# A gMLP and dilated-attention trunk on one core: combined weights and low halves moved to VectorE, a left operand read back from DRAM, attention steps moved out of the v stage

## The chip, the cores and the metric

The kernel runs on one core of a Trainium2 chip. The metric is the device time of one execution in microseconds (us). Five engines take part, each with an instruction stream of its own that runs in order: TensorE (PE; its weight loads are shown apart as PEld), VectorE (DVE), ScalarE (ACT), GpSimd (POOL), and SyncE (SP), which issues nearly all DMA transfers. Engines wait for each other through semaphores.

## The reference

The input is x, 2048 tokens by D = 1024, float32. There are two layers, cut here to what the kernel must compute:

```
h = rms_norm(x) * (1 + scale) + shift          # ada_mod(c) gives shift, scale, gate
u, v, z = split(h @ w_in, 3)                   # w_in: 1024 x 6144
v = rms_norm(gelu(v))
mixed = einsum('gts,bcsge->bctge', tril(w_s), v) + b_s    # inside chunks of 128 tokens
x1 = x + gate * ((gelu(u) * mixed * silu(z)) @ w_out)     # w_out: 2048 x 1024

k, v = split(norm(x1) @ w_kv)                  # one shared K/V, 6 heads of 128
q, z = norm(x1) @ w_in                         # 24 query heads, and 1024 columns of z
# three groups of 8 heads with dilation 1, 4 and 16, each over a band of 128 + own positions,
# with ALiBi slopes; the three outputs are weighed by softmax of their log-sum-exp
out = x1 + gate * ((sum_g alpha_g * o_g) * silu(z)) @ w_out
```

## The kernel before

**Tiling.** The tokens are worked in NQ = 4 quarters of QT = 512. A quarter runs `layer_A` (the gMLP layer) and then `proj_B` (K/V and queries of the attention layer); `finish` closes the last layer after the fourth quarter. `layer_A` has four stages, each of which keeps TensorE busy for 90 to 130 us: v, u, z and o (the product with w_out). Every float32 product is made of three TensorE products of high and low halves: `split` (L244) lets ACT copy a tile to its high half (L246) and another engine subtract that from the tile for the low half (L247). `mm3` (L275) issues the three.

**v in quarters 1 to 3** is made by `dense_s`, a Strassen-Winograd scheme with 7 products in place of 8 for each of two column blocks (numbers 4 and 5 of `block_of`). A product is 24 matmuls of 128x512 over four weight tiles, which `wunits` loads by SP and splits. The scheme needs combined weights (t1 to t4) and sums of the left operand (s1 to s4). `combine_weights` makes the former once, four 128x512 operations on POOL for each of 8 quads (L349 to L352), and stores them in DRAM (`wt`); for blocks 4 and 5 (`where="sums"`) this happens in quarter 0, mostly in the o stage. `sums_A` makes the latter: POOL adds the high and low halves of h, four tiles of 128x1024 (L610), DVE makes the sums (L614 to L617), and ACT and DVE split them into sA. In v the argument `shared=True` gives the low half of a product's fourth weight tile to POOL.

**h** itself is made by `norm_T` (names h_a, hAh, hAl) for the next quarter while `proj_B` runs; L489 writes it, L491 copies the high half, L493 (POOL) subtracts.

**Fillers.** Attention of the quarter before (`attend_local`, 80 steps) is a generator. The dense stages call `tick`, which advances the generators by `rate` steps for every full tick. The rate is 1.0 in v (16 ticks) and 1.5 or, in quarter 2, 1.6 in u, z and o (48 ticks); what is left is drained at the end of o. One attention visit is spread over four rounds: transposes of q and k (pq, pk), scores (ps, L1043 to L1049), transposes of the probabilities (pp, L1090 and L1104), and the product with v (po). Between scores and pp stand DVE's bias and maximum (L1052 to L1056), ACT's exponential (L1062) and POOL's diagonal, mask and copy (L1070 to L1073). In quarter 2 `ada_gate` "gb" (sums of a gate, DMA loads and DVE operations) is a second filler beside it.

**Order.** The tile framework's scheduler turns the program into one order per engine by priorities; engines and SP's queue then run in that order. The start of u also holds the scaling of v: eight DVE operations of 128x1024 (L780), each after a row factor rv from POOL, ahead of the mixing product pm (L787).

The line numbers in this document are those of the kernel before, unless a sentence says after: there a line stands one to five lower (L248 of after is L247, L351 to L354 are L349 to L352, L785 is L780, L1057 is L1052, L1095 is L1090).

Of the kernel before, what the change touches and what calls it, by code (L numbers as in the profile page):

```python
# [18 lines left out]
P = 128  # L19
# [15 lines left out]
def trunk(ctx, tc, out, x, c, a_ada_w, a_ada_b, a_norm_g, a_w_in, a_sgu_g, a_w_spatial,  # L35
# [27 lines left out]
    std = [dp.tile([S, 16], F32, name=f"std{g}") for g in range(3)]  # L63
    zd = dp.tile([S, D], F32, name="zd")
    gd = dp.tile([2, D], F32, name="gd")
    wt = [[dp.tile([512, 512], F32, name=f"wt{b}_{i}") for i in range(4)] for b in range(6)]

    fillers = []
# [172 lines left out]
        nc.gpsimd.tensor_tensor(t[:, 0:n], t[:, 0:n], mhalf[:, 0:n], ALU.pow)  # L241
        return t

    def split(hi, lo, src, e=None):  # L244

        nc.scalar.activation(hi, src, AF.Copy)  # L246
        (e or nc.vector).tensor_tensor(lo, src, hi.bitcast(F32), ALU.subtract)  # L247

    def wunits(w, k0, n0, nm, nk=KT, ordered=False, shared=False):
        us = []  # L250
        for kk in range(nk):
            u = wp.tile([P, 2, 512], F32R, tag="w", name=f"w_{nm}{kk}")
            raw = rp.tile([P, 512], F32, tag="raw", name=f"raw_{nm}{kk}")
            ld = nc.sync.dma_start(raw, w[(k0 + kk) * P:(k0 + kk + 1) * P, n0:n0 + 512])
            last_ld[0] = ld
            if ordered:
                tc.keep_in_program_order(ld)
            split(u[:, 0, :], u[:, 1, :], raw, nc.gpsimd if shared and kk == nk - 1 else None)
            us.append(u)
        return us  # L260

# [62 lines left out]
    def combine_weights(blocks, where):  # L324


        todo = [(b, k) for b in blocks for k in range(4)]
        quads = {}

        def load(i):  # L330
            b, k = todo[i]
            w, n0 = block_of(b)
            q = quads[i] = []
            for r in range(2):
                if where == "sums" or where == "both" and i % 2:
                    t = [sum_tile(f"cw{b}{k}{r}{c}")[:, 0:512] for c in range(2)]
                    for c in range(2):
                        nc.sync.dma_start(t[c], w[(4 * r + k) * P:(4 * r + k + 1) * P,
                                                  n0 + c * 512:n0 + (c + 1) * 512])
                else:  # L340
                    t = xp.tile([P, 2, 512], F32, tag="xin", name=f"cw{b}{k}{r}")
                    nc.sync.dma_start(t, w[(4 * r + k) * P:(4 * r + k + 1) * P, n0:n0 + D]
                                      .rearrange("p (c n) -> p c n", c=2))
                    t = [t[:, c, :] for c in range(2)]
                q += t

        def combine(i):
            t1, t3, t4, t2 = quads[i]
            nc.gpsimd.tensor_tensor(t1, t3, t1, ALU.subtract)  # L349
            nc.gpsimd.tensor_tensor(t3, t2, t3, ALU.subtract)  # L350
            nc.gpsimd.tensor_tensor(t2, t2, t1, ALU.subtract)  # L351
            nc.gpsimd.tensor_tensor(t4, t4, t2, ALU.subtract)  # L352

        def store(i):  # L354
            b, k = todo[i]
            t1, t3, t4, t2 = quads.pop(i)
            for j, t in enumerate((t1, t2, t3, t4)):
                nc.sync.dma_start(wt[b][j][k * P:(k + 1) * P, :], t)
            if k == 3:
                combined.add(b)  # L360

        for i in range(len(todo) + 2):
# [15 lines left out]
    def sum_tile(nm):  # L378
        return tp.tile([P, 520], F32, tag="st", name=f"st_{nm}")

    def dense_s(ops, b, nm, evac, late=None, shared=False):


        x, y = ([pst(f"pd_{nm}{c}{i}", "d") for i in range(2)] for c in "ab")
# [5 lines left out]
        src.update({f"t{i + 1}": (wt[b][i], 0, 0) for i in range(4)})  # L390

        def product(pts, a, w, first):
            us = wunits(*src[w], f"{nm}{w}_", 4, shared=shared)
# [76 lines left out]
    def norm_T(xts, pr, outs, nm, ks=range(0, KT, 2), act=False):  # L470

        tok = slice(pr * 256, pr * 256 + 256)
        pts = {}
        for oi, (hh, hl, a, b) in enumerate(outs):
            for k2 in ks:
                if oi == 0:
                    pts[k2] = pst(f"pt_{nm}{k2}").rearrange("p (k t) -> p k t", k=2)
                    for kk in range(2):
                        for i in range(2):
                            last = nc.tensor.transpose(pts[k2][:, kk, i * P:(i + 1) * P],  # L480
                                                       xts[i][:, (k2 + kk) * P:(k2 + kk + 1) * P], ident)
                h = evt(f"h_{nm}{k2}_{oi}").rearrange("p (k t) -> p k t", k=2)
                for kk in range(2):
                    k = k2 + kk
                    if act or (oi == 1):
                        nc.scalar.activation(h[:, kk, :], pts[k2][:, kk, :], AF.Identity,
                                             scale=a[:, k:k + 1], bias=b[:, k:k + 1])
                    else:
                        nc.vector.tensor_scalar(h[:, kk, :], pts[k2][:, kk, :], a[:, k:k + 1],  # L489
                                                b[:, k:k + 1], ALU.mult, ALU.add)  # L490
                nc.scalar.activation(hh[:, k2:k2 + 2, tok], h, AF.Copy)  # L491
                e = nc.vector if oi == 0 and len(outs) > 1 else nc.gpsimd
                e.tensor_tensor(hl[:, k2:k2 + 2, tok], h,  # L493
                                hh[:, k2:k2 + 2, tok].bitcast(F32), ALU.subtract)
        return last
# [100 lines left out]
    def sums_A(Q, hA, m):  # L596
# [9 lines left out]
            f[n] = m[1][:, i, :].rearrange("p (k t) -> p k t", k=4)  # L606
        for n in ("11", "21", "22", "12"):
            k, c = part[n]
            hi, lo = (h[:, k:k + 4, c:c + 256].bitcast(F32) for h in hA)
            nc.gpsimd.tensor_tensor(f[n], hi, lo, ALU.add)  # L610
        s = {"s1": f["22"], "s3": f["21"], "s2": f["11"], "s4": f["12"]}

        def sums():
# [761 lines left out]
```

## Time and profile before

| what | value |
|---|---|
| three runs | 3020.75, 3022.59, 3026.84 us (median 3022.59) |
| profiled execution, its own time | 3020.51 us |
| span of its profile | 3018.5 us |
| mean granted TensorE clock | 0.994 |
| v stage, quarters 1, 2, 3 (on TensorE) | 648 to 742, 1292 to 1391, 1967 to 2067 us |
| o stage of quarter 0 | 324 to 421 us |

The span is the time from the first to the last record; the profiled execution's own time holds 2.0 us more. The granted clock is the share of full speed that TensorE was allowed. A wait is idle time of an engine ahead of an instruction; the profile puts it down to the instruction that released it last ("A <- B" reads: A waited for B, or A is made from B).

### The profile page before, as it was taken

The numbers are of one execution on the slowest core, as the hardware profiler recorded it, in microseconds if no ns is written. First come the engines' busy times: TensorE is split into PE (matmuls) and PEld (weight loads), VectorE is DVE, ScalarE is ACT, GpSimd is POOL, SyncE is SP. The second block draws the span as 40 slices with busy tenths as digits, with TensorE's granted clock in tenths as the row PEclk, the third lists the DMA queues.
The fourth block names the chain that finished last, engine by engine and source line by source line (L and its number), as shares of the span: only waits on it lengthen the run. The fifth ranks groups of instructions, "written<-read, shape, count | busy, mean of one in ns | idle before, by whom it ended". The sixth has DMA issues, their size and how long they took to land. (4 is left out here: it accounts for less than half of the span.)

```text
span 3018.5 us, 45519 instructions
## 1 busy us (share of the span) xinstructions
PE 2937.2 (97%) x14752; PEld 2453.0 (81%) x14752; DVE 2125.0 (70%) x3714; ACT 1664.4 (55%) x3397; POOL 904.3 (30%) x1130
## 2 busy tenths in 40 slices
PE   7999999999999999999999999999999999999999
PEld 4788788878888888877888888878888888977787
DVE  5877566787557576887657686887577576878672
ACT  4323355768556365675445366576455366867440
POOL 1057422442003213643213213543123111122322
PEclk9999999999999999999999999999999999999999
DMA  8899865766343466765333366765433466788652
GB/s 275 274 310 346 295 229 180 254 218 194 120 130 102 126 200 213 254 219 164 107 121 124 116 199 210 252 195 158 131 101 106 133 194 203 235 279 293 214 168 91
DMA packets 363265, 583.49 MB, mean 193 GB/s; under 512 B 38442, under 2 KB 137996, under 8 KB 363028
## 3 DMA queue, kind: packets, MB, share of 16 engines
q1 hardware_dynamic: 363028, 580.59, 59.9%
q8 instruction: 117, 1.92, 0.3%
q14 instruction: 120, 0.98, 0.1%
HBM read 466.54 MB, written 113.91 MB: 192 GB/s over the span
## 5 line engine op out<-in xcount | busy, mean ns | idle before, releaser
L275 PE MATMUL pd_o<-w_o,yh 128*128 128x512 f32 x1024 | 322.1, 395 | 5.3 <-DVE w_o L247 5.3
L275 PE MATMUL pd_kv<-w_kv,hkh 128*128 128x512 f32 x768 | 239.1, 393 | 0.3
L275 PEld LDWEIGHTS pd_o<-w_o,yh 128*128 128x128 f32 x1024 | 190.7, 189 | 44.6 <-DVE w_o L247 6.3
L1062 ACT ACTIVATE pr<-pr,stat,rt 128x256 f32<-128x256 f32 (+1 forms) x320 | 177.6, 557 | 85.6 <-DVE stat L1059 54.3
L313 PE MATMUL pd_u<-hAh,w_u 128*128 128x512 f32 x512 | 206.7, 404 | 0.0
L313 PE MATMUL pd_z<-hAh,w_z 128*128 128x512 f32 x512 | 204.2, 399 | 0.0
L275 PE MATMUL pd_o<-w_o,yl 128*128 128x512 f32 x512 | 201.0, 393 | 0.0
L315 PE MATMUL pd_u<-hAh,w_u 128*128 128x512 f32 x512 | 200.4, 391 | 0.0
L315 PE MATMUL pd_z<-hAh,w_z 128*128 128x512 f32 x512 | 200.4, 391 | 0.0
L314 PE MATMUL pd_z<-hAl,w_z 128*128 128x512 f32 x512 | 199.8, 390 | 0.0
L314 PE MATMUL pd_u<-hAl,w_u 128*128 128x512 f32 x512 | 199.8, 390 | 0.0
L246 ACT ACTIVATE w_z<-raw_z 128x512 fp32r<-128x512 f32 x128 | 79.2, 628 | 173.4 <-PE pd_z L315 64.2
L275 PEld LDWEIGHTS pd_kv<-w_kv,hkh 128*128 128x128 f32 x768 | 143.0, 188 | 30.6 <-ACT hkh L519 2.0
L246 ACT ACTIVATE w_u<-raw_u 128x512 fp32r<-128x512 f32 x128 | 79.0, 629 | 160.9 <-PE pd_u L315 74.9
L246 ACT ACTIVATE w_o<-raw_o 128x512 fp32r<-128x512 f32 x128 | 79.2, 628 | 144.9 <-PE pd_o L275 66.2
L247 DVE TENSOR_TENSOR w_z<-raw_z,w_z 128x512 fp32r<-128x512 f32 x128 | 100.9, 797 | 78.0 <-ACT w_z L246 77.6
L1070 POOL TENSOR_TENSOR dg<-pr,ident 128x256 f32<-128x256 f32 x76 | 60.7, 798 | 314.3 <-ACT pr L1062 302.4
L1123 PEld LDWEIGHTS po<-kv,pT 128*128 128x128 f32 x1200 | 147.5, 192 | 8.1 <-ACT pT L970 1.6
L1123 PE MATMUL po<-kv,pT 128*128 128x128 f32 x1200 | 149.7, 275 | 1.0 <-ACT pT L970 1.0
L275 PE MATMUL pd_kv<-w_kv,hkl 128*128 128x512 f32 x384 | 149.6, 391 | 0.0
L247 DVE TENSOR_TENSOR w_o<-raw_o,w_o 128x512 fp32r<-128x512 f32 x128 | 100.9, 799 | 68.2 <-ACT w_o L246 68.1
L1052 DVE SCALAR_TENSOR_TENSOR pr<-dist,rt,ps 128x256 f32<-128x256 f32 (+1 forms) x320 | 122.6, 429 | 22.1 <-PE ps L1049 17.3
(837 smaller groups left out, 8177.0 us busy)
## 6 DMA issues: line engine op xcount, KB each, us to landing
raw_q<-in_b_w_in_dram SPq DMA_DIRECT2D x144, 256.0 KB, 3.3
raw_u<-in_a_w_in_dram SPq DMA_DIRECT2D x128, 256.0 KB, 3.6
raw_z<-in_a_w_in_dram SPq DMA_DIRECT2D x128, 256.0 KB, 3.3
raw_o<-in_a_w_out_dram SPq DMA_DIRECT2D x128, 256.0 KB, 3.0
qt<-qd SPq DMA_DIRECT2D x96, 260.0 KB, 3.2
raw_v<-in_a_w_in_dram SPq DMA_DIRECT2D x96, 256.0 KB, 4.0
raw_kv<-in_w_kv_dram SPq DMA_DIRECT2D x96, 256.0 KB, 3.1
od<-ot SPq DMA_DIRECT2D x96, 256.0 KB, 3.2
```

Source lines behind the costliest of these rows:

```text
L246: nc.scalar.activation(hi, src, AF.Copy)
L247: (e or nc.vector).tensor_tensor(lo, src, hi.bitcast(F32), ALU.subtract)
L275: last_mm[0] = nc.tensor.matmul(pt, a, u[:, w, :], start=f, stop=e, skip_group_check=more)
L313: nc.tensor.matmul(pts[i], wh, hh[:, k, :], start=k == 0, stop=False)
L314: nc.tensor.matmul(pts[i], wh, hl[:, k, :], start=False, stop=False)
L315: nc.tensor.matmul(pts[i], wl, hh[:, k, :], start=False, stop=k == KT - 1)
L1052: nc.vector.scalar_tensor_tensor(pr[:, i, :], dist[:, 256 - w:256], u["rt"][:, h:h + 1], psc[:, i, :], ALU.mult, ALU.add)
L1062: nc.scalar.activation(pr[:, i, :], pr[:, i, :], AF.Exp, bias=mneg[:, i:i + 1], scale=u["rt"][:, h:h + 1], accum_out=lsum[:, i:i + 1])
L1070: nc.gpsimd.tensor_tensor(dg, prev, ident.unsqueeze(1).broadcast_to([P, hp, P]), ALU.mult)
L1123: nc.tensor.matmul(po[:, h * P:(h + 1) * P], u["pT"][h // hp][:, h % hp, j, :], u["kv"][:, j, kh, 1, :], start=j == 0, stop=j == nk - 1)
```

## The change

Five things are changed. The combination of weights for blocks 4 and 5 runs on DVE; the blocks combined with `where="both"` stay on POOL. All low halves of v's weights are made on DVE. While `norm_T` makes h of a quarter from 1 on, SP stores each piece of h unsplit to a DRAM tile `hd` (8 stores of 256 KB a quarter), and `sums_A` reads four pieces of 512 KB back in place of POOL's four additions. The attention generator stands still in v (rate 0) and runs at 1.75 in u, z and o. `ada_gate` "gb" moves from quarter 2's v and u to quarter 1's u.

```diff
+    hd = dp.tile([2, P, KT, 256], F32, name="hd")
...
-    def split(hi, lo, src, e=None):
+    def split(hi, lo, src):
 
         nc.scalar.activation(hi, src, AF.Copy)
-        (e or nc.vector).tensor_tensor(lo, src, hi.bitcast(F32), ALU.subtract)
+        nc.vector.tensor_tensor(lo, src, hi.bitcast(F32), ALU.subtract)
...
-            split(u[:, 0, :], u[:, 1, :], raw, nc.gpsimd if shared and kk == nk - 1 else None)
+            split(u[:, 0, :], u[:, 1, :], raw)
...
         def combine(i):
             t1, t3, t4, t2 = quads[i]
-            nc.gpsimd.tensor_tensor(t1, t3, t1, ALU.subtract)
-            nc.gpsimd.tensor_tensor(t3, t2, t3, ALU.subtract)
-            nc.gpsimd.tensor_tensor(t2, t2, t1, ALU.subtract)
-            nc.gpsimd.tensor_tensor(t4, t4, t2, ALU.subtract)
+            e = nc.vector if where == "sums" else nc.gpsimd
+            e.tensor_tensor(t1, t3, t1, ALU.subtract)
+            e.tensor_tensor(t3, t2, t3, ALU.subtract)
+            e.tensor_tensor(t2, t2, t1, ALU.subtract)
+            e.tensor_tensor(t4, t4, t2, ALU.subtract)
...
                 nc.scalar.activation(hh[:, k2:k2 + 2, tok], h, AF.Copy)
+                if len(outs) == 1:
+                    nc.sync.dma_start(hd[pr, :, k2:k2 + 2, :], h)
...
         for n in ("11", "21", "22", "12"):
             k, c = part[n]
-            hi, lo = (h[:, k:k + 4, c:c + 256].bitcast(F32) for h in hA)
-            nc.gpsimd.tensor_tensor(f[n], hi, lo, ALU.add)
+            nc.sync.dma_start(f[n], hd[c // 256, :, k:k + 4, :])
...
-                dense_s(ops, 4 + b, f"v{Q}{b}", lambda t, src, n: ev[n](t, src[:, 0:512]), None if b else sums, True)
-            rate[0] = 1.6 if Q == 2 else 1.5
+                dense_s(ops, 4 + b, f"v{Q}{b}", lambda t, src, n: ev[n](t, src[:, 0:512]), None if b else sums)
+            rate[0] = 1.75
+            if Q == 1:
+                fillers.append(ada_gate(b_ada_w[0], b_ada_b, 1, "gb"))
...
             fillers.append(attend_local(Q - 1, True))
-            if Q == 2:
-                fillers.append(ada_gate(b_ada_w[0], b_ada_b, 1, "gb"))
-            rate[0] = 1.0
+            rate[0] = 0.0
```

Three places of the order follow, as the scheduler sets it. The first is DVE at the start of quarter 0's o stage. w_o are low halves of w_out's tiles (the first figure after o is the block, the last the tile), yl low halves of the left operand, mt the mixed and gated product it is made of, st_cw the quads of block 4. Before:

```order
L247 TENSOR_TENSOR w_o00_0_3_2853<-raw_o00_0_3_2854,w_o00_0_3_2853 128x512
L247 TENSOR_TENSOR w_o00_0_4_2858<-raw_o00_0_4_2859,w_o00_0_4_2858 128x512
L247 TENSOR_TENSOR w_o00_0_5_2863<-raw_o00_0_5_2864,w_o00_0_5_2863 128x512
L247 TENSOR_TENSOR w_o00_0_6_2868<-raw_o00_0_6_2869,w_o00_0_6_2868 128x512
L815 TENSOR_TENSOR yl04_2433<-mt0_1_1161,yh04_2432 128x512 x6
L812 TENSOR_TENSOR mt0_1_1161<-mt0_1_1161,z0_14_2808 128x512
L812 TENSOR_TENSOR mt0_1_1161<-mt0_1_1161,z0_15_2813 128x512
L247 TENSOR_TENSOR w_o00_0_7_2873<-raw_o00_0_7_2874,w_o00_0_7_2873 128x512
L815 TENSOR_TENSOR yl04_2433<-mt0_1_1161,yh04_2432 128x512 x2
```

After:

```order
L248 TENSOR_TENSOR w_o00_0_5_2864<-raw_o00_0_5_2865,w_o00_0_5_2864 128x512
L353 TENSOR_TENSOR st_cw4011_2910<-st_cw4011_2910,st_cw4000_2905 128x512
L351 TENSOR_TENSOR st_cw4100_2951<-st_cw4101_2952,st_cw4100_2951 128x512
L354 TENSOR_TENSOR st_cw4010_2909<-st_cw4010_2909,st_cw4011_2910 128x512
L248 TENSOR_TENSOR w_o00_0_6_2869<-raw_o00_0_6_2870,w_o00_0_6_2869 128x512
L352 TENSOR_TENSOR st_cw4101_2952<-st_cw4111_2956,st_cw4101_2952 128x512
L353 TENSOR_TENSOR st_cw4111_2956<-st_cw4111_2956,st_cw4100_2951 128x512
L820 TENSOR_TENSOR yl04_2434<-mt0_1_1162,yh04_2433 128x512 x6
L817 TENSOR_TENSOR mt0_1_1162<-mt0_1_1162,z0_14_2809 128x512
L817 TENSOR_TENSOR mt0_1_1162<-mt0_1_1162,z0_15_2814 128x512
L248 TENSOR_TENSOR w_o00_0_7_2874<-raw_o00_0_7_2875,w_o00_0_7_2874 128x512
L820 TENSOR_TENSOR yl04_2434<-mt0_1_1162,yh04_2433 128x512 x2
```

Parts of the combination now stand ahead of yl and of the last weight of the first block, w_o00_0_7; two more rows of it (L351 and L352 of after) stand right ahead of this piece.

The second is DVE where the z block of quarter 0's proj_B ends and v of quarter 1 begins. st_z0b are evacuations of the z block, m1_1 the pieces of h and their sums, sA the sums' low halves, w_v1011 and w_v1021 the weights of v's first and second product. Before:

```order
L407 TENSOR_TENSOR st_z0bw0_5863<-pd_z0ba0_5513,st_z0bu0_5573 128x512
L407 TENSOR_TENSOR st_z0bw1_5864<-pd_z0ba1_5514,st_z0bu1_5574 128x512
L247 TENSOR_TENSOR w_v1011_2_5951<-raw_v1011_2_5952,w_v1011_2_5951 128x512
L616 TENSOR_TENSOR m1_1_5926<-m1_1_5926 128x1024
L247 TENSOR_TENSOR sA10_5931<-m1_1_5926,sA10_5931 128x1024
L617 TENSOR_TENSOR m1_1_5926<-m1_1_5926 128x1024
L407 TENSOR_TENSOR st_z0bu0_5573<-pd_z0bb0_5515,st_z0bu0_5573 128x512
L407 TENSOR_TENSOR st_z0bu1_5574<-pd_z0bb1_5516,st_z0bu1_5574 128x512
L247 TENSOR_TENSOR sA10_5931<-m1_1_5926,sA10_5931 128x1024
L247 TENSOR_TENSOR sA11_5932<-m1_1_5926,sA11_5932 128x1024
L968 COPY kT1_0_5982<-pk1_0_5979 128x2x128
L247 TENSOR_TENSOR sA11_5932<-m1_1_5926,sA11_5932 128x1024
```

After:

```order
L248 TENSOR_TENSOR w_v1011_2_5960<-raw_v1011_2_5961,w_v1011_2_5960 128x512
L248 TENSOR_TENSOR w_v1011_3_5965<-raw_v1011_3_5966,w_v1011_3_5965 128x512
L409 TENSOR_TENSOR st_z0bu0_5578<-pd_z0bb0_5519,st_z0bu0_5578 128x512
L409 TENSOR_TENSOR st_z0bu1_5579<-pd_z0bb1_5520,st_z0bu1_5579 128x512
L619 TENSOR_TENSOR m1_1_5935<-m1_1_5935 128x1024
L248 TENSOR_TENSOR sA10_5940<-m1_1_5935,sA10_5940 128x1024
L620 TENSOR_TENSOR m1_1_5935<-m1_1_5935 128x1024
L248 TENSOR_TENSOR sA10_5940<-m1_1_5935,sA10_5940 128x1024
L248 TENSOR_TENSOR sA11_5941<-m1_1_5935,sA11_5941 128x1024 x2
L248 TENSOR_TENSOR w_v1021_0_6010<-raw_v1021_0_6011,w_v1021_0_6010 128x512
L248 TENSOR_TENSOR w_v1021_1_6015<-raw_v1021_1_6016,w_v1021_1_6015 128x512
L248 TENSOR_TENSOR w_v1021_2_6020<-raw_v1021_2_6021,w_v1021_2_6020 128x512
```

The low half of the first product's fourth weight (w_v1011_3) has come to DVE; the sums and low halves keep their order between the evacuation of z and the weights of the second product.

The third is PE in the first two blocks of u in quarter 2. pd_u are u's products, pm mixes v, pq transposes queries, pp transposes the probabilities of the first attention visit whose scores stand in u: visit 1_5 before, visit 1_4 after. Its scores stand ahead of these rows. Before:

```order
L313 MATMUL pd_u21_0_13120<-hAh2_10755,w_u214_13168 128x512
L314 MATMUL pd_u21_0_13120<-hAl2_10756,w_u214_13168 128x512
L315 MATMUL pd_u21_0_13120<-hAh2_10755,w_u214_13168 128x512
L313 MATMUL pd_u21_1_13121<-hAh2_10755,w_u214_13168 128x512
L314 MATMUL pd_u21_1_13121<-hAl2_10756,w_u214_13168 128x512
L315 MATMUL pd_u21_1_13121<-hAh2_10755,w_u214_13168 128x512
L1090 MATMUL pp1_5_0_13179<-ident_127,pr1_5_00_13007 128x128 x2
L1090 MATMUL pp1_5_0_13179<-ident_127,pr1_5_01_13025 128x128 x2
```

After:

```order
L792 MATMUL pm2_0_12976<-wst_192,m2_0_12069 128x128 x4
L792 MATMUL pm2_1_12985<-wst_192,m2_0_12069 128x128 x4
L314 MATMUL pd_u21_0_12994<-hAh2_10810,w_u210_12996 128x512
L315 MATMUL pd_u21_0_12994<-hAl2_10811,w_u210_12996 128x512
L316 MATMUL pd_u21_0_12994<-hAh2_10810,w_u210_12996 128x512
L314 MATMUL pd_u21_1_12995<-hAh2_10810,w_u210_12996 128x512
L315 MATMUL pd_u21_1_12995<-hAl2_10811,w_u210_12996 128x512
L316 MATMUL pd_u21_1_12995<-hAh2_10810,w_u210_12996 128x512
L1095 MATMUL pp1_4_0_13007<-ident_128,pr1_4_00_12904 128x128 x2
L1095 MATMUL pp1_4_0_13007<-ident_128,pr1_4_01_12922 128x128 x2
```

Before, pp stands two weight tiles later, behind products on w_u214, 66 rows behind the last score; after, it follows pm and six matmuls on w_u210, 28 rows behind the last score.

More of the change, by code (lines that the diff above doesn't have):

```diff
@@ L242, in rstd_of, with wunits @@
         return t
-    def split(hi, lo, src, e=None):
+    def split(hi, lo, src):
         nc.scalar.activation(hi, src, AF.Copy)
-        (e or nc.vector).tensor_tensor(lo, src, hi.bitcast(F32), ALU.subtract)
-    def wunits(w, k0, n0, nm, nk=KT, ordered=False, shared=False):
+        nc.vector.tensor_tensor(lo, src, hi.bitcast(F32), ALU.subtract)
+    def wunits(w, k0, n0, nm, nk=KT, ordered=False):
         us = []
@@ L379, in sum_tile, with dense_s @@
         return tp.tile([P, 520], F32, tag="st", name=f"st_{nm}")
-    def dense_s(ops, b, nm, evac, late=None, shared=False):
+    def dense_s(ops, b, nm, evac, late=None):
         x, y = ([pst(f"pd_{nm}{c}{i}", "d") for i in range(2)] for c in "ab")
@@ L392, in product @@
         def product(pts, a, w, first):
-            us = wunits(*src[w], f"{nm}{w}_", 4, shared=shared)
+            us = wunits(*src[w], f"{nm}{w}_", 4)
             store_late(5)
```

## The prediction

> **What bounds the kernel now.** I read the page's totals first, then the waits of TensorE over the whole run and stretch by stretch, then the granted clock by stretch, and last the timelines around the few places where TensorE stands still.
>
> ```profile
> span 3018.5 us, 45519 instructions
> PE 2937.2 (97%) x14752; PEld 2453.0 (81%) x14752; DVE 2125.0 (70%) x3714; ACT 1664.4 (55%) x3397; POOL 904.3 (30%) x1130
> ...
> PE pp L1090 <- POOL pr L1073: 8.2, 6, 2.4
> PE pd_o L275 <- DVE w_o L247: 5.3, 2, 5.1
> ```
>
> TensorE (PE) is busy 97% of the span; all other time is 81 us, in which a clock below full speed does not even show. The change removes no product, so it can only move PE's waits and its clock. The last two rows are two of its largest waits (total us, times, longest): the attention step for POOL's probabilities, and the output projection for a DVE low half.
>
> The v stages come next: their waits, first and last row of 6, 7 and 5, for 590 to 750, 1270 to 1400 and 1950 to 2070 us; then stretches (length, busy time and count of PE, PEld, DVE, ACT, POOL, then PE's granted clock, DMA share, GB/s).
>
> ```profile
> PE ps L1043 <- ACT qT L1014: 1.9, 1, 1.9
> ...
> PE pd_v10a L275 <- POOL w_v L247: 0.4, 1, 0.4
> PE pd_v20a L275 <- DVE st_z1bw L407: 3.1, 1, 3.1
> ...
> PE pd_v20b L275 <- POOL w_v20t L247: 0.7, 1, 0.7
> PE ps L1047 <- ACT qT L1016: 2.4, 1, 2.4
> ...
> PE pd_v30a L275 <- POOL w_v L247: 0.2, 1, 0.2
> 300.00:375.00 75.00, 69.90 (x297) 57.35 (x296) 44.03 (x47) 24.03 (x43) 35.15 (x24) 0.95 0.87 296
> 600.00:675.00 75.00, 69.19 (x314) 55.38 (x313) 65.40 (x85) 48.27 (x89) 34.96 (x33) 0.98 0.69 222
> 1275.00:1350.00 75.00, 68.15 (x302) 54.74 (x301) 62.76 (x91) 50.42 (x96) 29.21 (x21) 0.95 0.65 213
> 1350.00:1400.00 50.00, 46.80 (x212) 36.65 (x210) 36.49 (x64) 33.46 (x68) 20.73 (x17) 0.97 0.64 209
> 1950.00:2025.00 75.00, 69.54 (x333) 56.80 (x333) 66.23 (x98) 55.38 (x108) 35.68 (x29) 0.98 0.61 194
> ```
>
> The waits sum to 5.8, 10.1 and 5.3, together 21.2 us. The clock takes (1 - 0.98) x 75 = 1.5, 3.75 + 1.5 and 1.5, together 8.25 us. So v has 29.5 us to give, with DVE busy 84 to 88% there. The quarter-0 stretch has 5.1 us of wait and 0.05 x 75 = 3.75 us of clock.
>
> **Weight combination and quarter 0's output projection.** The rows are DVE's, POOL's and PE's in that order.
>
> ```profile
> 323.56 9.96 DVE L815 TENSOR_TENSOR yl<-mt,yh 128x512 fp32r<-128x512 f32 x6 [0.58 <-PE pd_z L314]
> 333.44 3.42 DVE L812 TENSOR_TENSOR mt<-mt,z 128x512 f32<-128x512 f32 x2
> 336.79 1.75 DVE L247 TENSOR_TENSOR w_o<-raw_o,w_o 128x512 fp32r<-128x512 f32 x1
> 344.40 0.69 DVE L247 TENSOR_TENSOR w_o<-raw_o,w_o 128x512 fp32r<-128x512 f32 x1 [2.50 <-ACT w_o L246]
> ...
> 321.12 1.31 POOL L349 TENSOR_TENSOR st_cw<-st_cw,st_cw 128x512 f32<-128x512 f32 x1 [21.42 <-DMA st_cw<-in_a_w_in_dram]
> 323.16 1.30 POOL L350 TENSOR_TENSOR st_cw<-st_cw,st_cw 128x512 f32<-128x512 f32 x1 [0.73 <-DMA st_cw<-in_a_w_in_dram]
> 327.84 1.73 POOL L349 TENSOR_TENSOR st_cw<-st_cw,st_cw 128x512 f32<-128x512 f32 x1
> ...
> 333.10 0.39 PE L275 MATMUL pd_o<-w_o,yh 128*128 128x512 f32 x1
> 338.59 0.79 PE L275 MATMUL pd_o<-w_o,yh 128*128 128x512 f32 x1 [5.10 <-DVE w_o L247]
> ```
>
> While POOL combines, DVE's 128x512 subtraction takes 9.96 / 6 = 1.66 us; with POOL idle it takes 0.69. The 32 POOL operations of some 1.7 us become 32 of 0.69 us on DVE: 22 us in a stage of 97 us where DVE is busy 44 of 75, so they find room. What counts is the order ahead of w_o7, which PE wants at 333.1. After the change six of the 32 stand between w_o5 and the yl block (4.1 us of work, paced by their loads: the first landed at 321.1, the next at 323.2, so I take the last for 326), then yl x6 and mt x2 at 0.69 (5.5 us) and w_o7 itself: 327 + 5.5 + 0.7 = 333.2. The wait all but goes. I leave 1 us of the 8.85: gain 7.9.
>
> A rule to weigh: the Trainium skill, page "SBUF — State Buffer", section "Who interferes with whom", says that a DVE instruction with both inputs in SBUF contends with a GpSimd instruction that reads SBUF. By that rule 1.66 falls to 0.69 wherever POOL's combination goes, which is the gain of 7.9; were 1.66 DVE's own price under DMA load, the block would end at 327 + 13.3 + 1.7 = 342, PE would wait 9 us instead of 5, and the sum below would come out 7.9 + 4 = 12 us higher.
>
> **v: low halves, read-back, sums.** The first three rows show DVE and POOL before v in quarter 1, the others the sums of the left operand and POOL's low halves.
>
> ```profile
> 623.70 9.29 DVE L247 TENSOR_TENSOR w_z0bt<-raw_z0bt,w_z0bt 128x512 fp32r<-128x512 f32 x4
> 637.61 0.99 DVE L489 TENSOR_SCALAR h_a<-pt_a,affa,affa 128x256 f32<-128x256 f32 x2
> 626.79 5.65 POOL L610 TENSOR_TENSOR m<-hAh,hAl 128x1024 f32<-128x1024 f32 x2
> 650.32 1.21 DVE L247 TENSOR_TENSOR sA<-m,sA 128x1024 fp32r<-128x1024 f32 x1
> 652.59 1.27 DVE L407 TENSOR_TENSOR st_z0bu<-pd_z0bb,st_z0bu 128x512 f32<-128x512 f32 x2
> 650.19 3.63 POOL L247 TENSOR_TENSOR w_v<-raw_v,w_v 128x512 fp32r<-128x512 f32 x1 [6.75 <-ACT w_v L246]
> raw_v<-in_a_w_in_dram SPq DMA_DIRECT2D x96, 256.0 KB, 4.0
> od<-ot SPq DMA_DIRECT2D x96, 256.0 KB, 3.2
> ```
>
> *Low halves.* 14 in each v go from POOL (up to 3.63 us) to DVE: 14 x 0.69 = 9.7 us per stage. Against them stand the contention they no longer make and the attention work of DVE that leaves the stage; I cost them at nothing. If that cover is gone, DVE's 84 to 88% becomes the bound: that is a rival below.
>
> *Read-back.* POOL loses 12 additions of 2.8 us. SP gains 24 stores of 256 KB and 12 reads of 512 KB: 4.2 MB a quarter. At the 222 GB/s of the 600 to 675 row that is 19 us of traffic, against 31% x 75 = 23 us of free DMA share. Bandwidth hides it; the order may not. The last h of quarter 1 is written by 638.6; its store lands 3.2 us later (as od<-ot), the last read, of twice raw_v's size, 4.0 to 5 us after that, at 646 to 647. On DVE the first two sums (2.3 us) then stand ahead of the third and fourth weight of v's first product, wanted 2.7 us after its start, some 651. That leaves 2 to 3 us of margin. SP meanwhile waits for the store with raw_v queued behind it; with one boundary in three late by 4 us plus 1.7 of clock, I charge 1.8 us. The bounds are 0 and 3 x 6 = 18 us.
>
> *Sums.* After the change DVE's order at the start of v is: two evacuations of the last z block (1.27), two more sums (1.14 each) and four 128x1024 low halves of sA (1.14 each), and only then the first weight of the second product: 1.27 + 6 x 1.14 + 0.69 = 8.8 us after PE finished z. The first product lasts 24 matmuls of 0.24 us = 5.7 us. PE waits 3 us in quarters 1 and 2 and, with one sum earlier, 1.5 in quarter 3: 7.0 us with rounding down, plus 2.5 us of clock and 0.5 of small waits. v keeps 7.0 + 2.5 + 0.5 + 1.8 = 11.8 of 29.5 us: gain 17.7. Upwards the term ends at 29.5; downwards at half of it, rival (3).
>
> **Attention out of v, denser elsewhere.** The rows are: the last score matmul, POOL's last step on its probabilities and PE's wait for them, at the start of u in quarter 3 and one visit later; and DVE's work at that start.
>
> ```profile
> 2063.70 3.01 PE L275 MATMUL pd_v31b<-w_v,sA 128*128 128x512 f32 x12
> 2066.55 0.39 PE L313 MATMUL pd_u<-hAh,w_u 128*128 128x512 f32 x1
> 2070.59 0.28 PE L1049 MATMUL ps<-kT,qT 128*128 128x256 f32 x1
> 2087.66 0.44 PE L1090 MATMUL pp<-ident,pr 128*128 128x128 f32 x2 [1.53 <-POOL pr L1073]
> ...
> 2091.99 0.28 PE L1049 MATMUL ps<-kT,qT 128*128 128x256 f32 x1
> 2074.41 4.07 DVE L780 TENSOR_SCALAR m<-m,rv 128x1024 f32<-128x1024 f32 x6 [1.10 <-POOL rv L241]
> 2086.34 1.26 POOL L1073 TENSOR_TENSOR pr<-pr 128x256 f32<-128x256 f32 x1
> 2100.50 0.74 POOL L1073 TENSOR_TENSOR pr<-pr 128x256 f32<-128x256 f32 x1
> ```
>
> From the last score matmul to the second finished probability tile the chain (DVE maximum, ACT exponential, POOL) takes 2101.24 - 2092.27 = 9.0 us in the ordinary visit and 2087.60 - 2070.87 = 16.7 us at the start of u, because DVE first scales m (L780). It ends 21 us after u begins. Matmuls of 0.23 us counted in the changed order put PE's transposes (pp) 9.1 to 12.2 us after the scores in most visits, where before they came 11.8 to 15.4 us after. So the ordinary visit still fits, by little. The start of u doesn't: in quarters 2 and 3 the scores end 8 and 6 us after u begins and the transposes stand at 15.0 and 15.5, with the m scaling still ahead on DVE. The chain there should end between 18 (9.0 us behind the end of L780, at 11.9, less what overlaps) and 21; I take 20, near the row of the same place: 4.5 us of stall and 1.4 of clock, twice, 11.8 us, less the 1.5 seen there: loss 10.3. First visits of the third dilation group, 7.3 us apart before and 7.3, 6.3 and about as much after, lose 1 us more, other visits 1, the drained remainder at the end of o and the kv weights loaded into shared buffers 2: loss 4 (0 to 9). The gate's column sums moved to quarter 1 only change which round they share; nothing, bounds -1 and 3.
>
> **Sum.** 3018.5 - 7.9 - 17.7 + 10.3 + 4.0 = 3007.2 us of span. The profiled execution took 2.0 us more than its span and lies 2.1 us under the median of the runs, 3022.59: 3011.3, say 3011.5. A measurement can tell about 0.2%, 6 us.
>
> Another rule to weigh: the Trainium skill, page "TensorE: Matmul & The Clock Gate", section "What's actually happening", says that the array halves its clock after an idle window of about 3.4 us. By it my 3 us stalls in v cost no clock and the sum is 2.5 us lower. The 0.95 of 1275 to 1350 us, where no listed wait is above 3.1, speaks against sparing it.
>
> **Rivals.** (1) Slower: the attention chain no longer fits. About 25 of the visits of three quarters stand at 9.1 to 10.9 us in the new order, against a chain of 9.0. It decides once DVE's extra work makes the chain 11.5 us, four low halves more ahead of a maximum: 25 x 1.1 = 28 us, in place of 2 of mine: 3037. For it: the chain was 16.7 once. Against: POOL has less to do, so its three steps come sooner. (2) Slower: the read-back is late at all three boundaries, 18.6 instead of 1.8: 3028. For it: store, read and SP's queue in series; against: the margin worked out above. (3) v doesn't empty: DVE, with 9.7 us more, still ends last there, and half the gain of v stays out: 3020, no change. (4) The u start fits, because the scores' own DVE steps come in ahead of m: 3001.
>
> **How the numbers follow.** My forecast has 0.45, rival (1) 0.18, (2) 0.12, (3) 0.13, (4) 0.12. The forecast's own range is 3003 to 3020, about a fifth of it above 3016.5. Faster by over 0.2%: 0.45 x 0.82 + 0.12 = 0.49; within: 0.08 + 0.10 = 0.18; slower: 0.18 + 0.12 + 0.03 = 0.33. The range for 8 in 10 reaches from 2996, below (4), to 3036, into (1).
>
> **What would show it.** Right: quarter 0's wait for w_o gone and DVE's yl at 0.7 us; v stages with waits below 4 us each, the longest for the first weight of the second product; new waits of 4 to 5 us for POOL's pr in the first 20 us of u in quarters 2 and 3. Wrong: many waits of 1 us for pr in u, z and o; waits in v that end with m<-hd; or a granted clock of 0.95 in several stretches that show 0.98 or more now.

## The result and the profile after

The changed kernel takes 3004.48 us (median of four runs, 3000.91 to 3006.91) against 3023.53 us before (3020.75 to 3026.84). The ratio is 0.9936 with a 95% interval of 0.9918 to 0.9953: 19 us faster, between 14 and 25. The forecast was 3011.5 us, 11 or 12 faster, with a range of 2996 to 3036.

The first two lines of the page, and the waits of TensorE over the whole run (total us, times, longest) that answer to those shown of before:

```profile
span 2998.9 us, 45673 instructions
PE 2931.3 (98%) x14752; PEld 2448.3 (82%) x14752; DVE 2106.8 (70%) x3788; ACT 1644.9 (55%) x3376; POOL 753.2 (25%) x1044
...
PE pk L1006 <- DMA kv<-kvd: 7.4, 1, 7.4
PE pp L1095 <- POOL pr L1078: 6.9, 7, 1.7
...
PE pd_v30b L276 <- ACT w_v30t L247: 2.7, 1, 2.7
...
PE pd_v10a L276 <- ACT st_v10u L415: 2.4, 1, 2.4
PE pd_o L276 <- DVE w_o L248: 2.2, 2, 1.2
```

POOL lost 151 us of work, DVE gained none in sum (2125.0 to 2106.8), although 74 instructions came to it: on average its instructions got shorter as POOL's left. Of the wait of 5.1 us in quarter 0's o stage two of 1.2 us and less are left, and a wait of 7.4 us has come that before did not have. The stretches (length, busy time and count of PE, PEld, DVE, ACT, POOL, granted clock, DMA share, GB/s) hold quarter 0's o stage and the starts of v in quarters 1 to 3:

```profile
295.00:370.00 75.00, 73.96 (x327) 60.89 (x326) 48.13 (x72) 26.52 (x48) 3.74 (x3) 1.00 0.91 310
590.00:665.00 75.00, 72.39 (x328) 59.20 (x327) 62.28 (x92) 48.51 (x84) 19.34 (x30) 0.98 0.86 290
1265.00:1340.00 75.00, 67.61 (x299) 55.59 (x298) 56.32 (x85) 50.82 (x93) 3.20 (x2) 0.95 0.81 267
1940.00:2015.00 75.00, 71.45 (x308) 58.35 (x307) 53.74 (x79) 52.60 (x98) 1.29 (x1) 0.95 0.76 244
```

In quarter 0 the clock is whole. At the three starts of v it takes 1.5 + 3.75 + 3.75 = 9.0 us, where the same starts of before lost 1.5 + 3.75 + 1.5 = 6.75 us. Over the whole of v the two kernels are equal: in each trace the granted clock stands at half for 17.1 us of the three v stages, which is 8.5 us lost.

To see where the time went, I took in both traces the time from each TensorE instruction's start to the next one's, less the median of its kind in the same trace, and summed that excess by stage. It holds waits, clock loss and what is hidden in matmuls that end late, and depends little on how many attention steps a stage holds. It does depend on what is taken for one kind: by shape alone v's difference comes out at -6.4 and that of z, o and kv at +1.0, so a row is good to some 2.5 us.

| excess on TensorE, us | before | after | difference | forecast |
|---|---|---|---|---|
| o stage of quarter 0 | 8.1 | 3.0 | -5.1 | -7.9 |
| z blocks of proj_B ahead of v, three | 12.2 | 2.5 | -9.7 | } -17.7 |
| v, quarters 1 to 3 | 29.4 | 20.6 | -8.8 | } |
| u, quarters 1 to 3 | 12.5 | 18.5 | +6.0 | +10.3 |
| z, o and the first kv block after it | 22.2 | 24.7 | +2.5 | +4.0 |
| everything else | 71.3 | 67.6 | -3.7 | 0 |

The sum is -18.8 of the span's -19.6. "Everything else" is mostly code that the change doesn't touch; in the fourteen traces of this study it lies between 64.6 and 71.7, so some 3 us either way may be one execution's chance.

### The profile page after: what moved, and what is told of

Same layout as the page of the kernel before. It is cut to its first block, busy times and chain, and to the rows that moved or that the text cites. A ratio compares the mean times of both kernels' runs of the same rounds, so it can differ in the third digit from the quotient of the medians.

```text
span 2998.9 us, 45673 instructions
## 1 busy us (share of the span) xinstructions
PE 2931.3 (98%) x14752; PEld 2448.3 (82%) x14752; DVE 2106.8 (70%) x3788; ACT 1644.9 (55%) x3376; POOL 753.2 (25%) x1044
## 5 line engine op out<-in xcount | busy, mean ns | idle before, releaser
L1128 PEld LDWEIGHTS po<-kv,pT 128*128 128x128 f32 x1200 | 147.3, 192 | 11.1 <-ACT pT L975 1.9
L248 DVE TENSOR_TENSOR w_u<-raw_u,w_u 128x512 fp32r<-128x512 f32 x128 | 94.7, 748 | 57.4 <-ACT w_u L247 57.2
```

The lines of the kernel that those rows point to most:

```text
L248: nc.vector.tensor_tensor(lo, src, hi.bitcast(F32), ALU.subtract)
L1128: nc.tensor.matmul(po[:, h * P:(h + 1) * P], u["pT"][h // hp][:, h % hp, j, :], u["kv"][:, j, kh, 1, :], start=j == 0, stop=j == nk - 1)
```

## Experiments: each part alone

Four kernels put one part of the change on the kernel before.

**The read-back alone.**

```diff
+                    nc.sync.dma_start(hd[pr, :, k2:k2 + 2, :], h)
...
-            nc.gpsimd.tensor_tensor(f[n], hi, lo, ALU.add)
+            nc.sync.dma_start(f[n], hd[c // 256, :, k:k + 4, :])
```

> The kernel before with the read-back alone: SP stores h and reads the four pieces, POOL's twelve additions (L610) are gone, all else as before. Theory A (POOL's additions held up DVE's splits in the z block ahead of each v, so their going is what shortened the three z blocks by 3.3, 3.5 and 2.5 us): the z blocks shorten by about 3 us each, the time falls by 8 to 12 us. Rival B (the gain there came from attention leaving v): the z blocks stay at 43.5 to 44.5 us and the time moves by under 3 us. Rival C (the read-back is late at the start of v, as the prediction's second rival had it): waits of 4 us and more at the starts of v, time up by 5 us or more.

Measured: ratio 0.9984 (0.9975 to 0.9993), 5 us faster. The three z blocks fell from 43.9, 44.5 and 43.5 us to 40.5, 41.0 and 40.5, their excess from 12.2 to 2.2: theory A's mechanism. But v's excess rose from 29.4 to 36.5 (quarter 1 +2.4, quarter 3 +4.8), which took most of it back (though one trace's v can differ by 4.5 us without cause, as the third kernel shows); theory A's size (8 to 12 us) was missed. The mechanism is seen in the splits of the z block, which before stood at 9.29 us for four beside POOL's additions. This kernel's rows for DVE at the same place:

```profile
618.15 1.36 DVE L248 TENSOR_TENSOR w_z0bt<-raw_z0bt,w_z0bt 128x512 fp32r<-128x512 f32 x2 [0.23 <-ACT w_z0bt L247]
626.78 2.06 DVE L248 TENSOR_TENSOR w_z0bt<-raw_z0bt,w_z0bt 128x512 fp32r<-128x512 f32 x2
```

They take 0.7 to 1.0 us each instead of 2.3, and TensorE in the z block no longer runs behind them.

**The attention out of v alone.**

```diff
-            rate[0] = 1.6 if Q == 2 else 1.5
+            rate[0] = 1.75
...
-            rate[0] = 1.0
+            rate[0] = 0.0
```

> The kernel before with the attention steps moved out of v (rates 0 and 1.75) and the gate's sums moved to quarter 1, all else as before. Theory A: v loses its waits for qT and its DVE work, but u, z and o give some 8 us back; time within 5 us of before. Rival B (attention in v was the whole cost): time down by 12 us or more, and the z blocks ahead of v 3 us shorter.

Measured: 0.9969 (0.9957 to 0.9981), 9 us faster, between the two theories. By stages v's excess falls from 29.4 to 21.9, the z blocks' from 12.2 to 9.9, while u gains 4.6 and z, o and kv 2.5: a net of 2.7 us. Another 5.5 us come from quarter 0's o stage (8.1 to 2.6), which this part does not touch. Up to the start of v in quarter 1 the order of this kernel's instructions on every engine is that of the kernel before (SP's last transfers ahead of that v apart), and still the stage took 91.4 us instead of 96.9. Its DVE and POOL rows point at the reason:

```profile
323.63 6.99 DVE L817 TENSOR_TENSOR yl<-mt,yh 128x512 fp32r<-128x512 f32 x6
...
324.88 1.79 POOL L350 TENSOR_TENSOR st_cw<-st_cw,st_cw 128x512 f32<-128x512 f32 x1 [1.88 <-DMA st_cw<-in_a_w_in_dram]
```

POOL's second operand landed 1.7 us later than in the profile of before, so POOL stood still for 1.88 us, and in that time some of DVE's subtractions can have run at their own speed: the six took 6.99 us, not 9.96. Whether this lateness belongs to the executions or to where this program's data lie is open.

**The combination alone.**

```diff
-            nc.gpsimd.tensor_tensor(t1, t3, t1, ALU.subtract)
+            e = nc.vector if where == "sums" else nc.gpsimd
+            e.tensor_tensor(t1, t3, t1, ALU.subtract)
...
```

> The kernel before with the combination for blocks 4 and 5 on DVE, all else as before. By the prediction's term for quarter 0's o stage it gains 5 us (the changed kernel's o stage was 91.9 us against 96.9), 2 more if what its profile still shows there comes from elsewhere. A rival is that only together with the other parts the order comes out so; then 0.

Measured: 0.9990 (0.9982 to 0.9999), 3 us faster. The stage took 92.0 us with an excess of 3.2, as in the changed kernel. In the same trace v's excess is 33.9, 4.5 above before, with v unchanged: so large is the chance in one trace's v.

**The low halves alone.**

```diff
-                dense_s(ops, 4 + b, f"v{Q}{b}", lambda t, src, n: ev[n](t, src[:, 0:512]), None if b else sums, True)
+                dense_s(ops, 4 + b, f"v{Q}{b}", lambda t, src, n: ev[n](t, src[:, 0:512]), None if b else sums)
```

> The kernel before with the 42 low halves of v's weights on DVE, all else as before. With the attention steps still in v, DVE (84 to 88% busy there) gets 14 x 0.69 = 9.7 us more a stage. Theory A: DVE ends last more often, v lengthens by 1 to 4 us a quarter, time up by 3 to 10 us. Rival B: POOL's 3.6 us on the last weight was worse than a place in DVE's queue; time down by 2 to 6 us.

Measured: 0.9962 (0.9950 to 0.9974), 12 us faster: more than either said, and the largest of the four for a part that the prediction had costed at nothing. TensorE's waits around v of quarter 2 in this kernel:

```profile
PE pd_v20b L275 <- ACT w_v20t L246: 3.0, 1, 3.0
PE pd_v20a L275 <- DVE st_z1bw L407: 2.0, 1, 2.0
PE pd_z1ba L275 <- DVE st_z1bv L407: 0.5, 1, 0.5
PE pd_v20a L275 <- ACT st_v20u L413: 0.4, 1, 0.4
```

They sum to 5.9 us instead of 10.1; the waits for POOL's w_v are gone, and with them one for DVE's st_v21v, which stood in the kernel before as:

```profile
PE pd_v21a L275 <- DVE st_v21v L407: 2.0, 1, 2.0
...
PE pd_v21a L275 <- POOL w_v21t L247: 1.2, 1, 1.2
...
PE pd_v20b L275 <- POOL w_v20t L247: 0.7, 1, 0.7
```

The excess of that stage falls from 14.7 to 8.5, that of u behind it from 5.3 to 3.8; quarters 1 and 3 show none of it. The profiled execution lies some 4 us above the median of this kernel's runs, so that the trace doesn't hold the whole gain, and where the rest of the 12 us lies is open.

Alone the four parts gave 5, 9, 3 and 12 us, together 29. The whole gave 19.

## Experiments: each part undone

Four kernels take one part out of the changed kernel. Edits are those above, backwards.

> The changed kernel with the read-back undone: POOL adds the halves of h again, no stores and reads of h. By the parts run alone: the three z blocks get 3 us longer each (contention of POOL's additions with DVE's splits), and v, whose sums then don't wait for the read, gets 2 to 5 us shorter in quarters 2 and 3. Theory: time up by 2 to 7 us. Rival: the two cancel, or the late read in quarter 2 (wait of 7.4 us) weighs more: no change or some us faster.

> The changed kernel with the attention steps and the gate's sums where they were before (rate 1.0 in v, 1.5 or 1.6 behind). Alone this part gave 9 us, and the three others alone gave 5, 3 and 12, more together than the 19 of the whole. Theory A: attention in v and low halves on POOL got in each other's way, either part removes the same waits; with the low halves on DVE the steps in v cost little, time within 4 us of the changed kernel's. Rival B: DVE now is too full in v (low halves, sums and attention): v 4 us longer a quarter, time up by 6 to 12 us in spite of u, z and o that get 8 us back.

> The changed kernel with the combination for blocks 4 and 5 back on POOL. The o stage of quarter 0 was 95.2 to 96.9 us in three kernels with POOL's combination, 91.4 in a fourth whose loads came 3 us later, and 89.2 to 92.0 in the six with DVE's. Theory: that stage takes 91 to 97 us, the time rises by 1 to 6 us. Rival: what the stage loses is made good behind it, as it is long before the end: 0.

> The changed kernel with one part undone: the 42 low halves of v's fourth weights go back to POOL. Alone on the kernel before that part gave 11 to 12 us, which the prediction had costed at nothing. Theory: POOL's slow subtraction (up to 3.63 us beside DVE's) was what v waited for, with or without the other parts: the time rises by 7 to 12 us. Rival: with POOL's additions and the attention gone from v, POOL and DVE no longer get in each other's way, and DVE's burst is shorter: within 3 us, or a few us faster.

| kernel | ratio to before (95%) | o, quarter 0 | z blocks | v | u | z, o, kv |
|---|---|---|---|---|---|---|
| before | 1 | 8.1 | 12.2 | 29.4 | 12.5 | 22.2 |
| changed | 0.9936 (0.9918 to 0.9953) | 3.0 | 2.5 | 20.6 | 18.5 | 24.7 |
| POOL's additions back | 0.9938 (0.9924 to 0.9953) | 0.8 | 8.0 | 20.8 | 17.1 | 24.7 |
| attention back in v | 0.9927 (0.9915 to 0.9939) | 0.7 | 2.2 | 30.5 | 10.6 | 23.8 |
| combination back on POOL | 0.9934 (0.9921 to 0.9948) | 7.1 | 2.5 | 17.6 | 19.1 | 24.9 |
| low halves back on POOL | 0.9934 (0.9918 to 0.9950) | 1.3 | 2.5 | 21.3 | 16.3 | 24.8 |

No single part is needed for most of the gain. The intervals are 4 to 5 us wide on either side, and a difference of two such ratios is good to 6 or 7 us; so a cost of some 4 to 8 us remains possible for each part, but not the 9 and 12 that two of them gave alone. The stages say how. Attention back in v costs v 10 us and gives u, z and o 9 back: moving it moves the waits along with it (theory A's time, though not by its reason: v did get longer, as B had it). The low halves on POOL cost nothing once no attention is in v: in that case POOL has nothing else to do there. Alone on the kernel before, the same 42 instructions stood in one queue with POOL's attention steps, and next to DVE's. So the two parts that gave most alone remove in part the same waits: either of them alone shortened quarter 2's v, from an excess of 14.7 us to 8.5 (low halves) and 5.4 (attention). That the shared queue is the reason is argued from the order; no run separates it from DVE's part. The additions and the combination do show in their own stages (z blocks 8.0, o stage 7.1, against 2.5 and 3.0), as their theories said, but 4 to 5 us did not reach the time beyond its interval, which neither confirms nor rules out the 2 to 7 and 1 to 6 us that they expected. Of the z blocks only two got longer again (43.5 and 43.4 us); quarter 3's, where POOL's additions came later, stayed at 41.0.

## Experiments: the two waits that the prediction named

**The sums at the start of v.** The prediction had DVE's burst of sums ahead of the second product's weights as what is left in v. In quarter 1 it was ACT's half of the same burst that came last. The changed kernel's ACT and PE rows:

```profile
643.15 2.94 ACT L247 ACTIVATE sA<-m 128x1024 fp32r<-128x1024 f32 x3
646.00 1.06 ACT L415 ACTIVATE st_v10u<-pd_v10a 128x512 f32<-128x512 f32 x2
...
646.62 0.60 PE L276 MATMUL pd_v10a<-w_v,hAh 128*128 128x512 f32 x1 [2.37 <-ACT st_v10u L415]
```

The second product adds to the accumulator that ACT must copy out first, and the copy stood behind three high halves of sums. In quarter 2 the order on SP, DVE, ACT and PE was this:

```profile
1280.99 0.38 SPq L613 DMA_DIRECT2D m<-hd  x1
1291.27 0.44 SPq L989 DMA_DIRECT2D kv<-kvd  x1
...
1286.25 1.23 DVE L617 TENSOR_TENSOR m<-m 128x1024 f32<-128x1024 f32 x1 [0.71 <-DMA m<-hd]
1293.26 3.48 DVE L248 TENSOR_TENSOR sA<-m,sA 128x1024 fp32r<-128x1024 f32 x3
1296.67 2.49 DVE L248 TENSOR_TENSOR w_v<-raw_v,w_v 128x512 fp32r<-128x512 f32 x4
...
1294.66 1.06 ACT L415 ACTIVATE st_v20u<-pd_v20a 128x512 f32<-128x512 f32 x2
...
1282.50 0.61 PE L276 MATMUL pd_v20a<-w_v,hAh 128*128 128x512 f32 x2
1295.49 0.45 PE L1006 MATMUL pk<-ident,kv 128*128 128x128 f32 x1 [7.39 <-DMA kv<-kvd]
```

SP issued the last read of h 1.5 us before v began, behind z's stores; the data came at 1286.25, 3.75 us into v. DVE's sums followed, and the first weight of the second product was split only at 1297.3. PE had finished the first product at 1288. The wait is put down to the attention's keys, which the scheduler had drawn forward into v and whose load stood late on SP too; but the other rows show that without it PE would have waited almost as long: ACT's first copy of the accumulator, behind the high halves of the sums as in quarter 1, ended only at 1295.2 us, and PE went on at 1295.5. The edit that tests it moves one line:

```diff
-            late()
             product(x, "12", "21", False)
             for i in range(2):
                 evac(i, x[i], 0)
+            late()
```

> The changed kernel, with the sums of the left operand called after v's second product in place of its first (the first use of a sum is in the fourth). Theory: in v of quarters 1 to 3 PE waits, right after the first product, for the burst of four sums and four low halves on DVE and ACT ahead of the second product's weights (in the changed kernel's trace 2.5, 7.4 and 2.8 + 1.2 us, with 1.7 to 3.4 us of half clock behind each). The burst moved, the three v stages lose about 3, 6 and 4 us and the time is 10 to 14 us under the changed kernel's: about 2991. Rival: the burst only makes the fourth product wait in place of the second; time within 3 us of the changed kernel's. Rival: the wait in quarter 2 is for the attention's keys, behind SP's queue, and stays; then 5 to 7 us less.

Measured: 0.9905 (0.9892 to 0.9919), 2991.2 us: 29 us under the kernel before, and by the ratios 9 under the changed one (13 by the medians, which stand beside different runs of before). It beats the kernel before clearly; its interval and that of the changed kernel just touch. The expected gain, 10 to 14 us with 13 of it in v, was not reached by the ratios: v's excess falls by 6.4, from 20.6 to 14.2. In this kernel's quarter 2 DVE reaches the second product's weights among the sums and not behind them, and the waits of that stretch are 3.6 us instead of 7.4. The last four rows are the waits at the starts of v in quarters 2, 1 and 3:

```profile
1283.46 0.68 DVE L248 TENSOR_TENSOR w_v<-raw_v,w_v 128x512 fp32r<-128x512 f32 x1
1285.30 1.22 DVE L619 TENSOR_TENSOR m<-m 128x1024 f32<-128x1024 f32 x1
...
PE pd_v20b L276 <- ACT w_v20t L247: 2.0, 1, 2.0
PE pd_v20a L276 <- ACT st_v20u L415: 1.6, 1, 1.6
PE pd_v10b L276 <- ACT w_v10t L247: 2.0, 1, 2.0
PE pd_v30b L276 <- ACT w_v30t L247: 2.9, 1, 2.9
```

The first rival fell (no wait before the fourth product took its place), and so did the second: the wait for the keys went as well, as the scheduler no longer put them ahead of that product. But in part the stall only moved on, to the third product's weights: in quarters 1 and 3 TensorE waited 2.5 and 3.4 us in all, hardly less than the 2.6 and 3.6 of the changed kernel, and what these quarters gained is clock. Nor is quarter 2 the edit's alone: the last read of h came 0.7 us into v here, not 3.75. Of the 9 us the trace places 6.4 in v; 2.6 lie in quarter 0's o stage, where the edit doesn't reach.

With the low halves on POOL in addition:

> The kernel with the later sums (2991 us), and the low halves of v's fourth weights on POOL in addition, where in the changed kernel they made no difference. Theory: no attention is in v, POOL is idle, DVE is relieved of 9.7 us a stage; equal or up to 5 us faster than with the later sums alone. Rival: with the sums out of the way DVE has room and POOL's subtraction beside DVE's (1.3 to 3.6 us) is the later one: 2 to 6 us slower.

Measured: 0.9899 (0.9885 to 0.9913), 2993.9 us. v's excess is 12.4. No difference from the later sums alone that can be told. Against the changed kernel with the low halves on POOL (0.9934, 21.3 us of excess in v) the later sums gave 11 us here, 8.9 of them in v: a second trial of the same edit.

**The start of u.** The changed kernel's rows for DVE, POOL and PE in quarter 2, where u begins at 1368.8:

```profile
1375.81 4.07 DVE L785 TENSOR_SCALAR m<-m,rv 128x1024 f32<-128x1024 f32 x6 [1.26 <-POOL rv L242]
...
1387.21 0.72 POOL L1078 TENSOR_TENSOR pr<-pr 128x256 f32<-128x256 f32 x1
...
1385.85 0.44 PE L1095 MATMUL pp<-ident,pr 128*128 128x128 f32 x2 [0.88 <-ACT pr L1067]
1387.99 0.69 PE L1095 MATMUL pp<-ident,pr 128*128 128x128 f32 x2 [1.70 <-POOL pr L1078]
```

DVE scales v until 11.1 us after the start, and the second probability tile is done at 19.1. PE came to its transposes at 16.2 and waited 2.6 us in two pieces. To take the cause away, the steps begin after u's first block, at a higher rate:

```diff
-            rate[0] = 1.75
...
         for j in range(8):
+            if Q and j == 1:
+                rate[0] = 1.83
```

> The changed kernel, with the attention steps starting after u's first block (11 us) at a rate of 1.83 in place of 1.75. Theory: the waits at u's start (2.9 us in quarter 2 with 1.7 us of half clock, 2.7 in quarter 3) are for probabilities that DVE makes only after it has scaled v; started later they go, and the time falls by 4 to 7 us. Rival: the higher rate makes the later visits wait as much: within 3 us.

Measured: 0.9953 (0.9939 to 0.9966), 3005.7 us: nothing gained, if anything some lost. u's excess fell from 18.5 to 11.6, as the theory said, and that of z, o and kv rose from 24.7 to 32.8. Of TensorE's waits in this kernel, over the whole run:

```profile
PE pp L1097 <- POOL pr L1080: 7.3, 8, 2.2
...
PE pp L1097 <- ACT z L817: 3.2, 1, 3.2
```

The total for POOL's probabilities is what it was (6.9 before this edit), only elsewhere, and one of 3.2 us at the start of o in quarter 2 is new. The rival holds: the wait moved.

This kernel, in which no key stands in v, also settles what v's second product waits for:

```profile
PE pd_v30a L276 <- ACT st_v30u L415: 4.4, 1, 4.4
PE pd_v20a L276 <- ACT st_v20u L415: 3.9, 1, 3.9
...
PE pd_v10a L276 <- ACT st_v10u L415: 3.0, 1, 3.0
```

In all three quarters it is ACT's copy of the accumulator.

Both edits together:

> Both edits on the changed kernel: the sums after the second product, and the attention from u's second block on at 1.83. If the two waits are what they are taken for, the gains add: 14 to 20 us under the changed kernel, about 2987. If the attention's start had been hidden by something else, no more than the later sums alone give.

Measured: 0.9929 (0.9917 to 0.9941), 2998.0 us, 7 above the later sums alone, with intervals that barely touch. v's excess is 12.3 and u's 11.6, z, o and kv 34.7. By the stages the second edit costs 9 us in z and o and saves 5 in u. Against the later attention alone, the later sums gave 7 us and took v's excess from 19.2 to 12.3: a third trial. The three waits for ACT's copy are down to 0.6, 0.7 and 2.1 us.

## Why the prediction was right, and where it was not

*Direction and place.* The net was right in sign and too small: 11 us forecast, 19 measured. By the table, measured less forecast is +2.8 us in quarter 0, -0.8 in v with its z blocks, -4.3 in u and -1.5 in z and o; -3.7 us lie where no term was, and may be chance.

*Quarter 0's o stage (forecast 7.9).* The mechanism stood. The changed kernel's DVE rows of that place:

```profile
327.29 3.69 DVE L820 TENSOR_TENSOR yl<-mt,yh 128x512 fp32r<-128x512 f32 x6
332.11 0.68 DVE L248 TENSOR_TENSOR w_o<-raw_o,w_o 128x512 fp32r<-128x512 f32 x1
```

Six subtractions take 3.69 us, not 9.96, and w_o7 is done at 332.8; 333.2 was worked out. DVE's own price is 0.62 to 0.69 us, and the 1.66 was POOL's doing: the rule of the Trainium skill ("SBUF — State Buffer", "Who interferes with whom") and the rows agree. The size was off: 5.1 us in the trace and 3 in the times of that part alone (0 to 5), since two waits of 1.2 us and less stayed. The stall of before is not in every profile, either: of five kernels with POOL's combination four show it at 4.4 to 5.1 us and one at 2.2. In the recorded sum, five of the 32 operations and w_o6 stand between w_o5 and yl, not six of the 32; the 4.1 us are the same.

*v (forecast 17.7 with its z blocks, 18.5 in the trace).* Right in sum by luck, with the parts mixed up. More than half came from the z blocks ahead of v, where POOL's additions slowed DVE's splits. The prediction showed the row for that (9.29 us for four) and did not price it; the stretches from which it took its 29.5 us counted only waits of TensorE and clock loss, and of the z blocks' 12.2 us these showed little. For the same reason v kept more than the 11.8 us that were left to it, 20.6. The low halves, "costed at nothing", were worth 12 us alone and nothing that can be told in the whole: the contention was named as cover, and its price was not looked for.

*The stall for the sums (forecast 3, 3 and 1.5 us).* It is there: moving it gave 9, 11 and 7 us in three pairs of kernels, 6.4 to 8.9 of them in v, clock included, where 7.0 were forecast and 2.5 of clock. What ended last was another engine's work: ACT's copy of the accumulator and not DVE's split; in quarter 2 the late read seems to have made it longer.

*The read-back (forecast 1.8 us, one boundary in three late).* One of three was late, quarter 2's, through SP: the read stood behind z's stores, which waited for ACT. The second rival therefore happened at one place only, as part of a wait of 7.4 us, where the forecast had 4 us and 1.7 of clock for such a boundary.

*The start of u (forecast 10.3).* The place and cause were right, the size was twice too big: 2.6 us where 4.5 were forecast in quarter 2. The chain ended at 19.1 us, not 20, and PE came at 16.2, not 15.0, as matmuls counted at 0.23 us left out the transposes between them. The difference of two times with an error of 1 us each was the whole term.

*Rivals.* The attention chain (first rival) did not outgrow its spacing: z, o and kv lost 2.5 us in all, not 28. DVE in v (third) was not the bound: it was busy 56 of 75 us there in quarter 2, less than before. The fourth, that the start of u fits, would have given 3001; the measured time lies between it and the forecast. The second's 3028 us is 0.18% above the time before, so its chance belonged under "within" and not under "slower".

*The clock.* Here a step failed outright: 2.5 us of clock were left to v, and 8.5 are there over its three stages, as before, so that nothing came back. Each of the three starts of v still had one stall of over 2 us, and one such stall can be enough: in quarter 1 TensorE stood still for 2.4 us, and for 3.4 us behind it the clock stood at half, which is 1.7 us lost. It need not be: with the later sums a stall of 2.9 us at the start of v in quarter 3 left the clock whole, where one of 2.7 us in the changed kernel was followed by 6.8 us at half. What decides between them no run shows. One of the signs of being wrong came: from 1940 to 2015 us the clock is 0.95, where the start of the same v showed 0.98 before. The rule of an idle window of about 3.4 us (the Trainium skill, "TensorE: Matmul & The Clock Gate", "What's actually happening"), taken as a threshold on a single gap, does not hold here; the decision to charge clock for shorter stalls was right, and the charge too small.

## What to carry to other kernels

When two engines slow each other down, the price stands in the duration of single instructions beside and without the neighbour, not in the waits of the engine that is the bound; price it there, and look for it in every stage where both run, also ahead of the one that is changed. A step that is needed only three products later should not be issued in front of the next product's weights: moving one line behind one product gave about half as much again as the whole change, though part of that stall only moved on to the next weights. Parts of a change that remove the same waits do not add, so a part should be judged alone and undone, and a stall, or a loss of clock, of one profiled execution should be checked against a second one before it is counted whole.

## What the runs showed of the hardware

A DVE subtraction of 128x512 with both operands on chip took 0.62 to 0.69 us alone, 1.66 beside POOL's 128x512 subtraction and 2.3 beside its 128x1024 addition; POOL's own went from 1.3 to 1.6 or 1.8. Programs with the same order of instructions showed the same stage at 91.4 and at 96.9 us; in the shorter one a load had landed 1.7 us later, and POOL stood still beside DVE's first subtractions. A stall of TensorE of 2.4 us was followed by 3.4 us at half clock in one place, and one of 2.9 us by none in another.
